# Differential scores with grouped 64-row products, and projections whose arithmetic leaves GpSimd

## Chip, cores and metric

One core of a Trainium2 chip runs the whole kernel. The metric is device microseconds from launch to end. The time before is 1314.98 us, the median of three runs (1313.61 to 1316.22); the execution that was profiled took 1315.7 us.

## The reference, cut to what matters

One layer of a transformer block on 1024 tokens of 1024 columns, in float32. The part around the change:

```python
h = rms_norm(x, norm_mix)
q_lat, kv_lat, k_rope_in, dq, dk, dv, g_mla, g_diff = split(h @ w_in)
# latent attention (8 heads): q and k get a norm with a gain, 32 of 96 columns are rotated
q = rms_norm(rms_norm(q_lat) @ w_uq, q_gain);  k = rms_norm(concat(k_nope, k_rope), k_gain)
# differential attention (4 heads, 2 halves of 64 columns): 16 of 64 columns are rotated
q = rms_norm(dq.reshape(4, 2, 64), q_gain);  k = rms_norm(dk.reshape(4, 2, 64), k_gain)
p1 = softmax(q1 @ k1.T * scale);  p2 = softmax(q2 @ k2.T * scale)   # chunk-causal, blocks of 128 queries
o = rms_norm((p1 - lam * p2) @ v, subln)
# then gates, up-projections, w_out, a router and 32 experts (top 2 in one group)
```

## The kernel before, in words

Every product of two float32 matrices is made of rounded parts (`split`, line 81): ScalarE copies the operand to the rounded type (`hi`), another engine takes the remainder (`lo`), and three products (`mm3`, line 85) are summed in PSUM: hi x hi, hi x lo, lo x hi. A *remainder* below is the TENSOR_TENSOR of line 83. `split` does it on VectorE unless it is given GpSimd; `load_split` (line 148) gives GpSimd all weight pieces but the first, and lines 419 and 422 give it those of `w_uq` and `w_ukv`.

The kernel runs in stages. **Projections** (0 to 285 us): the transposed input is loaded in two halves of tokens (`load_hT`), the norm of each token comes from squares of x (`norm_x`, line 170), and the eight token tiles of the differential queries are made first, into eight PSUM banks (`first`): tiles 0 and 1 share one tile of the pool psA, 2 and 3 the other; tile 4 is in bank "g". `diff_proj` (line 268) empties a bank: a square on ScalarE, a sum over each of 16 half-heads and an inverse root by a Newton step on VectorE, then scaling and rotation. For queries (c = 0) it reads the bank with the product of both gains (`gdqk`, line 285) and with rotary tables (`rope`, line 241, lines 246 to 250), and the norm is applied at the end by GpSimd (line 288). For keys (c = 1) VectorE applies the norm while it reads the bank (lines 293 and 294). Then a loop over tiles (line 426) makes the latents (`lat_proj`, in bank "g" from tile 1 on), the values (`dv_proj`), the latent queries and keys (`prep`, where GpSimd applies the queries' norm in line 401) and their transposes (`turn`, line 255, through PSUM and one ScalarE copy to DRAM). A second loop (line 446) does the differential keys.

**Latent attention** (299 to 487 us) and **differential attention** (487 to 687 us) follow. For each head and block i of 128 queries `diff_scores` (line 637) makes two score matrices of (i + 1) x 128 keys, one for each half f. The halves lie in partitions 0 to 63 and 64 to 127. The first product of a half has 128 rows (hi and lo of the query stacked against hi of the key, line 655), the second one 64 rows (hi of the query against lo of the key, line 656), and up to 512 columns each: one column piece for i below 4, two from there on. For i below 4 both halves lie in one psA tile, from i = 4 on each takes a psA tile of its own; the pool has two. VectorE masks a corner and takes the row maximum (lines 657 and 511), ScalarE the exponential (line 514). Scores are made two blocks ahead of their use; products of the gates (`gates`, lines 86 to 88 with `pG`) are dealt out as filler by `filler`.

What stands in an engine's queue, and in which order, is settled when the kernel is built: a scheduler takes the program's order as priority and a model of times, so that a later instruction whose operands and buffers are free in its model passes an earlier one whose buffer is not.

After 687 us come the output projection, the router and the experts, which the change does not touch.

Of the kernel before, what the change touches and what calls it, by code (L numbers as in the profile page):

```python
# [10 lines left out]
F32 = mybir.dt.float32  # L11
# [4 lines left out]
AF = mybir.ActivationFunctionType  # L16
ALU = mybir.AluOpType
# [7 lines left out]
P = 128  # L25
KD = 8
MH, MN, MR, MV, MQK = 8, 64, 32, 64, 96
# [4 lines left out]
LAMBDA_INIT = 0.8 - 0.6  # L32
NEG = -1e30
N_RAW = 5
SPV = (0,)
XB = 4
XTB = 4
NGB = 4
# [10 lines left out]
def kernel(ctx: ExitStack, tc: tile.TileContext, a, out):  # L49
    nc = tc.nc  # L50
# [97 lines left out]
    def load_split(src, n):  # L148
        i = next(raws)
        raw = er(i)[:, :n]  # L150
        nc.sync.dma_start(raw, src)
        hi = pw.tile([P, 1024], F32R, name="whi", bufs=6)
        lo = pw.tile([P, 1024], F32R, name="wlo", bufs=6)
        split(hi[:, :n], lo[:, :n], raw, None if i in SPV else nc.gpsimd)
        return hi, lo

    gT = p1.tile([P, KD], F32, name="gT")
# [37 lines left out]
    for k2 in range(4):  # L195
        w_dq.append(w_piece(a["w_dqkv"][0], 512, k2))
        for k in (2 * k2, 2 * k2 + 1):
            load_hT(k, 0)
            for t in range(4):
                proj(first[t], t, w_dq, 512, k, k + 1)  # L200
    for k in range(KD):
        load_hT(k, 1)
    norm_x(0, 4)
    norm_x(4, NT)
    first += [bank(x) for x in ("g", "o", "", "")]
    for k in range(KD):
# [34 lines left out]
    def rope(dst, src, tab, t, nh, h, r0):  # L241

        tmp = p1.tile([P, 2, 256], F32, name="rtmp", bufs=2)
        m = [tmp[:, i, :nh * 2 * h].rearrange("p (n h) -> p n h", h=2 * h) for i in range(2)]
        for m_, x in zip(m, tab):
            nc.vector.tensor_tensor(m_, src[:, :, r0:r0 + 2 * h], x[:, t:t + 1, :].to_broadcast([P, nh, 2 * h]),  # L246
                                    op=ALU.mult)
        mc, ms = m
        nc.vector.tensor_tensor(dst[:, :, r0:r0 + h], mc[:, :, :h], ms[:, :, h:], op=ALU.subtract)
        nc.vector.tensor_tensor(dst[:, :, r0 + h:r0 + 2 * h], mc[:, :, h:], ms[:, :, :h], op=ALU.add)  # L250

    def work(name, shape, dt=F32, bufs=2):
        return p1.tile(shape, dt, name=name, bufs=bufs)

    def turn(pool, srcs, dsts, w):

        pt = bank2()
        n = [x.shape[-1] // w for x in srcs]
        for j, (x, b) in enumerate((x, b) for x, n_ in zip(srcs, n) for b in range(n_)):
            nc.tensor.transpose(pt[:w, j * P:(j + 1) * P], x[:, b * w:(b + 1) * w], ident)  # L260
        o = pool.tile([P, KD, P], F32, name="to", bufs=2)
        nc.scalar.activation(o[:w], pt[:w, :].rearrange("p (h n) -> p h n", n=P), AF.Copy)
        h = 0
        for (d_, t_), n_ in zip(dsts, n):
            nc.sync.dma_start(d_[:, :, t_ * P:(t_ + 1) * P], o[:w, h:h + n_, :])
            h += n_

    def diff_proj(c, t, w, ps=None):
        if ps is None:
            ps = bank(("g", "")[t % 2])  # L270
            proj(ps, t, w, 512)
        r_ = rx[:, t:t + 1]
        o = work("v", [P, 512]) if c else px.tile([P, 512], F32, name="v0", bufs=4)
        sq = work("sq", [P, 512], bufs=1)
        nc.scalar.activation(sq, ps, AF.Square, scale=r_)
        ss = work("ss8", [P, 8])
        nc.vector.tensor_reduce(ss, sq.rearrange("p (h d) -> p h d", d=DHD), axis=AX, op=ALU.add)
        r8 = work("r8", [P, 8])
        rstd_newton(p1, r8, ss, DHD)
        src = ps.rearrange("p (h d) -> p h d", d=DHD)  # L280
        ov = o.rearrange("p (h d) -> p h d", d=DHD)
        if c == 0:
            rs = work("rs8", [P, 8])
            nc.vector.tensor_scalar(rs, r8, r_, DHD ** -0.5, op0=ALU.mult, op1=ALU.mult)
            nc.vector.tensor_tensor(ov[:, :, DR:], src[:, :, DR:],
                                    gdqk[:, None, DR:].to_broadcast([P, 8, DHD - DR]), op=ALU.mult)
            rope(ov, src, tdq, t, 8, 8, 0)
            nc.gpsimd.tensor_tensor(ov, ov, rs[:, :, None].to_broadcast([P, 8, DHD]), op=ALU.mult)
            nc.sync.dma_start(dqr_d[t * P:(t + 1) * P, :], o)
        else:  # L290
            nc.vector.tensor_scalar(r8, r8, r_, None, op0=ALU.mult)
            kn = work("kn", [P, 8, DR])
            nc.vector.tensor_tensor(kn, src[:, :, :DR], r8[:, :, None].to_broadcast([P, 8, DR]), op=ALU.mult)
            nc.vector.tensor_tensor(ov[:, :, DR:], src[:, :, DR:],
                                    r8[:, :, None].to_broadcast([P, 8, DHD - DR]), op=ALU.mult)
            rope(ov, kn, tdk, t, 8, 8, 0)
        return o

    gdqk = p1.tile([P, DHD], F32, name="gdqk")
    nc.vector.tensor_tensor(gdqk, gdq, gdk, op=ALU.mult)  # L300
    tdq = tables("tdq", gdq, cd, sd, 0, 8)
    tdk = tables("tdk", gdk, cd, sd, 0, 8)
    for t in range(NT):
        diff_proj(0, t, w_dq, first[t])
    es_x.close()

    gqk = p1.tile([P, MN], F32, name="gqk")
    nc.vector.tensor_tensor(gqk, gq[:, :MN], gk[:, :MN], op=ALU.mult)
    tq = tables("tq", gq, cm, sm, MN, 16)
    tk = tables("tk", gk, cm, sm, MN, 16)  # L310

# [55 lines left out]
    def prep(t):  # L367
# [25 lines left out]
        rstd_newton(p1, r16, ss, MQK)  # L393
        nc.vector.tensor_scalar(r16[:, :8], r16[:, :8], MQK ** -0.5, None, op0=ALU.mult)
        q = pp.tile([P, MH, MQK], F32, name="q", bufs=1)
        for h0, h1, o in ((0, 5, 0), (5, 8, 512)):
            src = pq[:, o:o + (h1 - h0) * MQK].rearrange("p (h d) -> p h d", d=MQK)
            nc.vector.tensor_tensor(q[:, h0:h1, :MN], src[:, :, :MN],
                                    gqk[:, None, :].to_broadcast([P, h1 - h0, MN]), op=ALU.mult)
            rope(q[:, h0:h1, :], src, tq, t, h1 - h0, 16, MN)  # L400
        nc.gpsimd.tensor_tensor(q, q, r16[:, :8, None].to_broadcast([P, MH, MQK]), op=ALU.mult)
        kk = pp.tile([P, MH, MQK], F32, name="k", bufs=1)
        rk = r16[:, 8:16, None]
        nc.vector.tensor_tensor(kk[:, :, :MN], pk.rearrange("p (h d) -> p h d", d=MN),
                                rk.to_broadcast([P, MH, MN]), op=ALU.mult)
        nc.vector.scalar_tensor_tensor(kk[:, :, MN:], kr.to_broadcast([P, MH, MR]), rx[:, t:t + 1],
                                       rk.to_broadcast([P, MH, MR]), op0=ALU.mult, op1=ALU.mult)
        QK[t] = ((q, q_d), (kk, k_d))

    QK = {}  # L410

    def prep_t(t):
        for x, d_ in QK.pop(t):
            turn(pp, [x.rearrange("p h d -> p (h d)")], [(d_, t)], MQK)

    for k in range(2):
        raw = er(next(raws))[:, :768]
        nc.sync.dma_start(raw, a["w_uq"][:, k, :])
        split(uqh[:, k, :], uql[:, k, :], raw, nc.gpsimd)
    raw = er(next(raws))  # L420
    nc.sync.dma_start(raw, a["w_ukv"])
    split(ukh, ukl, raw, nc.gpsimd)
    w_dv = dv_pieces(0)
    early = [bank2()]
    early = [x[:, o:o + 512] for o in (0, 512) for x in early]
# [20 lines left out]
    for t in range(NT):  # L446
        dk = diff_proj(1, t, w_dk)
        dv_proj(1, t, w_dv, bank("o"))
        if t:
            turn(pt_, [fetch("dqr", dqr_d, t - 1, 2), dk_], [(dq_d, t - 1), (dk_d, t - 1)], P)  # L450
        dk_ = dk
    turn(pt_, [fetch("dqr", dqr_d, t, 2), dk_], [(dq_d, t), (dk_d, t)], P)
    es_1.close()
    es_w.close()

# [181 lines left out]
    def diff_scores(m):  # L637

        h, i = divmod(m, NT)
        qs, ks, kl, _ = HD["d", h]  # L640
        n = (i + 1) * P
        ps = bank2()
        if i < 4:
            ps, cuts = [ps[:, :512], ps[:, 512:]], [slice(0, n)]
        else:
            (p0, cuts), (p1, _) = score_banks(ps, i), score_banks(bank2(), i)
            ps = [p0, p1]
        r_ = pa.tile([P, 2], F32, name="rd", bufs=4)
        s_ = pa.tile([P, 2], F32, name="sd", bufs=4)
        p = []  # L650
        for f in range(2):
            c = slice(f * 64, f * 64 + 64)
            q = qs[f][:, i * P:(i + 1) * P]
            for k in cuts:
                nc.tensor.matmul(ps[f][:, k], q, ks[f][:, k], start=True, stop=False)
                nc.tensor.matmul(ps[f][:, k], q[c], kl[c, k], start=False, stop=True)
            nc.vector.memset(ps[f][0:64, n - 64:n], NEG)
            p.append(softmax_exp(pa, ps[f], n, f"d{f}", s_[:, f:f + 1])[0])
        nc.vector.reciprocal(r_, s_)
        p_1, r_1 = p[0], r_[:, 0:1]  # L660
# [587 lines left out]
```

## Time and profile before

| | |
|---|---|
| median of three runs | 1314.98 us |
| the profiled execution | 1315.7 us |
| its span, first to last instruction | 1313.6 us |
| TensorE busy | 1193.0 us (91%) |
| VectorE busy | 943.8 us (72%) |
| ScalarE busy | 735.1 us (56%) |
| GpSimd busy | 233.0 us (18%) |

In the profile's rows PE is TensorE, PEld its weight loads, DVE VectorE, ACT ScalarE, POOL GpSimd. L83 is line 83 of the kernel. A row of a line names what it writes and reads. Matmul ends are modelled and overlap with the next one, so the distance between starts says what a product costs. [...]

### The profile page before, as it was taken

The numbers are of one execution on the slowest core, as the hardware profiler recorded it, in microseconds if no ns is written. First come the engines' busy times: TensorE is split into PE (matmuls) and PEld (weight loads), VectorE is DVE, ScalarE is ACT, GpSimd is POOL, SyncE is SP. The second block draws the span as 40 slices with busy tenths as digits, with TensorE's granted clock in tenths as the row PEclk, the third lists the DMA queues.
The fourth block names the chain that finished last, engine by engine and source line by source line (L and its number), as shares of the span: only waits on it lengthen the run. The fifth ranks groups of instructions, "written<-read, shape, count | busy, mean of one in ns | idle before, by whom it ended". The sixth has DMA issues, their size and how long they took to land. (4 is left out here: it accounts for less than half of the span.)

```text
span 1313.6 us, 18269 instructions
## 1 busy us (share of the span) xinstructions
PE 1193.0 (91%) x6105; PEld 954.1 (73%) x6105; DVE 943.8 (72%) x2071; ACT 735.1 (56%) x1368; POOL 233.0 (18%) x175
## 2 busy tenths in 40 slices
PE   7769969999999999999999899999599989899994
PEld 6668858877888886666778678888477756666773
DVE  5487685447888887877675678445679878878992
ACT  5444443246676675766565444211478767677882
POOL 2341050010000001101010000000154434342111
PEclk9889979999999999999999999999689989999997
DMA  8843346475233323313114443754569999999993
GB/s 263 200 155 116 105 124 173 122 154 121 78 92 94 88 81 113 102 60 96 65 33 137 152 144 113 267 181 169 199 194 342 309 311 303 327 317 343 341 319 56
DMA packets 107423, 228.61 MB, mean 174 GB/s; under 512 B 13793, under 2 KB 47201, under 8 KB 107329
## 3 DMA queue, kind: packets, MB, share of 16 engines
q1 hardware_dynamic: 86272, 201.98, 46.1%
q0 software_dynamic: 21056, 25.46, 9.6%
q8 instruction: 49, 0.80, 0.3%
q14 instruction: 46, 0.37, 0.1%
HBM read 187.53 MB, written 52.43 MB: 183 GB/s over the span
## 5 line engine op out<-in xcount | busy, mean ns | idle before, releaser
L83 DVE TENSOR_TENSOR elo<-ring,ehi 128x1024 fp32r<-128x1024 f32 x120 | 141.8, 1220 | 16.2 <-ACT ehi L82 15.9
L82 ACT ACTIVATE ehi<-ring 128x1024 fp32r<-128x1024 f32 x120 | 124.8, 1058 | 33.9 <-DMA ring<-in_w_exp 16.6
L514 ACT ACTIVATE pd<-pA,nbd 128x512 f32<-128x512 f32 (+7 forms) x128 | 94.7, 740 | 33.9 <-DVE nbd L511 33.0
L86 PE MATMUL pG<-ring,whi 128*128 128x512 f32 x240 | 101.2, 422 | 4.0 <-ACT sg L488 3.8
L511 DVE TENSOR_REDUCE nbd<-pA 128x1 f32<-128x128 f32 (+7 forms) x128 | 95.7, 748 | 4.1 <-PE pA L562 3.5
L87 PE MATMUL pG<-ring,whi 128*128 128x512 f32 x240 | 97.3, 406 | 0.0
L88 PE MATMUL pG<-ring,wlo 128*128 128x512 f32 x240 | 97.0, 404 | 0.0
L83 DVE TENSOR_TENSOR elo<-er,ehi 128x1024 fp32r<-128x1024 f32 x72 | 85.5, 1220 | 9.7 <-ACT ehi L82 9.5
L82 ACT ACTIVATE ehi<-er 128x1024 fp32r<-128x1024 f32 x72 | 75.0, 1058 | 21.4 <-DMA er<-in_w_exp 8.0
L1083 POOL DMA_INDIRECT out<-y,ids x22 | 54.1, 2457 | 143.3 <-DVE elo L83 30.6
L86 PE MATMUL pG<-ehi,xh 128*112 128x512 f32 x128 | 53.0, 414 | 20.5 <-ACT xh L82 20.5
L523 PE MATMUL pB<-ident,pd 128*128 128x128 f32 x432 | 66.5, 278 | 1.3 <-DVE pt L83 0.2
L86 PEld LDWEIGHTS pG<-ring,whi 128*128 128x128 f32 x240 | 46.2, 193 | 16.5 <-ACT sg L488 7.0
L523 PEld LDWEIGHTS pB<-ident,pd 128*128 128x128 f32 x432 | 48.9, 141 | 12.3 <-issue 2.6
L86 PE MATMUL pG<-whi,ring 128*128 128x416 f32 (+1 forms) x96 | 37.5, 391 | 21.5 <-DVE rtmp L246 20.8
L88 PE MATMUL pB<-ehi,ehl 128*112 128x512 f32 x128 | 54.7, 427 | 1.8 <-DVE ehl L83 1.8
L86 PE MATMUL pB<-ehi,ehh 128*112 128x512 f32 x128 | 54.8, 428 | 0.9 <-DVE y L1082 0.7
L82 ACT ACTIVATE whi<-er 128x512 fp32r<-128x512 f32 (+2 forms) x48 | 36.0, 758 | 31.0 <-PE pG L87 11.6
L88 PEld LDWEIGHTS pG<-ring,wlo 128*128 128x128 f32 x240 | 46.0, 192 | 10.0 <-issue 0.4
L87 PE MATMUL pB<-elo,ehh 128*112 128x512 f32 x128 | 53.0, 414 | 0.0
L88 PE MATMUL pG<-ehi,xl 128*112 128x512 f32 x128 | 52.0, 406 | 0.0
L87 PEld LDWEIGHTS pG<-ring,whi 128*128 128x128 f32 x240 | 46.2, 192 | 7.6 <-issue 1.0
(391 smaller groups left out, 3569.0 us busy)
## 6 DMA issues: line engine op xcount, KB each, us to landing
ring<-in_w_exp SPq DMA_DIRECT2D x120, 512.0 KB
er<-in_w_exp SPq DMA_DIRECT2D x72, 512.0 KB
er<-in_w_gate SPq DMA_DIRECT2D x16, 512.0 KB
g_d<-sg SPq DMA_DIRECT2D x32, 256.0 KB
sgl<-g_d SPq DMA_DIRECT2D x32, 256.0 KB
er<-in_w_dqkv SPq DMA_DIRECT2D x8, 512.0 KB
xT<-in_xT SPq DMA_DIRECT2D x16, 256.0 KB
xt<-in_x SPq DMA_DIRECT2D x8, 512.0 KB
```

Of the source, the lines that this page charges most:

```text
L82: nc.scalar.activation(hi, src, AF.Copy)
L83: (eng or nc.vector).tensor_tensor(lo, src, hi, op=ALU.subtract)
L86: nc.tensor.matmul(ps, ah, bh, start=start, stop=False)
L87: nc.tensor.matmul(ps, ah, bl, start=False, stop=False)
L88: nc.tensor.matmul(ps, al, bh, start=False, stop=stop)
L511: nc.vector.tensor_reduce(nb, ps[:, :n], axis=AX, op=ALU.max, negate=True)
L514: nc.scalar.activation(p[:, :n], ps[:, :n], AF.Exp, bias=nb, accum_out=s)
L523: nc.tensor.transpose(pt[:, (b - b0) * P:(b - b0 + 1) * P], p[:, b * P:(b + 1) * P], ident)
L1083: nc.gpsimd.indirect_dma_start(out=out[:, :], out_offset=bass.IndirectOffsetOnAxis(ap=idx[:BT, :], axis=0), in_=y[:BT, :], in_offset=None, ...
```

## The change

Two changes are put together.

In `diff_scores` the 128-row products of both halves come first, then the 64-row products, in turn for half 0 and half 1 of each column piece; mask and softmax of both halves follow all products.

In the projections no arithmetic is given to GpSimd any more. All weight remainders go to VectorE. `diff_proj` reads queries the way it reads keys: the norm is applied while the bank is read, with a copy `kn` (now one buffer) of the 16 columns to be rotated. `prep` does the same with `qn`, and rotates eight heads at once. The product of both gains for the columns that are not rotated becomes a column (`gain_column`, small loads on GpSimd's DMA queue) and is the scale of the ScalarE copy in `turn`; for the differential part that copy becomes two, one for queries and one for keys. `norm_x(0, 4)` comes ahead of the second half of `load_hT`.

```diff
-SPV = (0,)
...
-        split(hi[:, :n], lo[:, :n], raw, None if i in SPV else nc.gpsimd)
+        split(hi[:, :n], lo[:, :n], raw)
...
+    norm_x(0, 4)
     for k in range(KD):
         load_hT(k, 1)
-    norm_x(0, 4)
     norm_x(4, NT)
...
-            nc.vector.tensor_tensor(m_, src[:, :, r0:r0 + 2 * h], x[:, t:t + 1, :].to_broadcast([P, nh, 2 * h]),
-                                    op=ALU.mult)
+            nc.vector.tensor_tensor(m_, src, x[:, t:t + 1, :].to_broadcast([P, nh, 2 * h]), op=ALU.mult)
...
+    def gain_column(nm, gains, cuts, n):
+
+        col_ = p1.tile([P, 2], F32, name=f"{nm}2")
+        nc.vector.memset(col_, 1.0)
+        for i, g_ in enumerate(gains):
+            for p0, d0, d1 in cuts:
+                nc.gpsimd.dma_start(col_[p0:p0 + d1 - d0, i:i + 1], a[g_][d0:d1].rearrange("(p o) -> p o", o=1))
+        r = p1.tile([P, 1], F32, name=nm)
+        nc.vector.tensor_tensor(r[:n], col_[:n, 0:1], col_[:n, 1:2], op=ALU.mult)
+        return r
+
-    def turn(pool, srcs, dsts, w):
+    def turn(pool, srcs, dsts, w, gains):
...
-        nc.scalar.activation(o[:w], pt[:w, :].rearrange("p (h n) -> p h n", n=P), AF.Copy)
         h = 0
-        for (d_, t_), n_ in zip(dsts, n):
+        for (d_, t_), n_, g_ in zip(dsts, n, gains):
+            src = pt[:w, h * P:(h + n_) * P].rearrange("p (h n) -> p h n", n=P)
+            if g_ is None:
+                nc.scalar.activation(o[:w, h:h + n_, :], src, AF.Copy)
+            else:
+                nc.scalar.activation(o[:w, h:h + n_, :], src, AF.Copy, scale=g_[:w])
             nc.sync.dma_start(d_[:, :, t_ * P:(t_ + 1) * P], o[:w, h:h + n_, :])
...
+        nc.vector.tensor_scalar(r8, r8, r_, DHD ** -0.5 if c == 0 else 1.0, op0=ALU.mult, op1=ALU.mult)
+        kn = work("kn", [P, 8, DR], bufs=1)
+        nc.vector.tensor_tensor(kn, src[:, :, :DR], r8[:, :, None].to_broadcast([P, 8, DR]), op=ALU.mult)
+        nc.vector.tensor_tensor(ov[:, :, DR:], src[:, :, DR:],
+                                r8[:, :, None].to_broadcast([P, 8, DHD - DR]), op=ALU.mult)
+        rope(ov, kn, (tdk if c else tdq), t, 8, 8, 0)
         if c == 0:
-            rs = work("rs8", [P, 8])
-            nc.vector.tensor_scalar(rs, r8, r_, DHD ** -0.5, op0=ALU.mult, op1=ALU.mult)
-            nc.vector.tensor_tensor(ov[:, :, DR:], src[:, :, DR:],
-                                    gdqk[:, None, DR:].to_broadcast([P, 8, DHD - DR]), op=ALU.mult)
-            rope(ov, src, tdq, t, 8, 8, 0)
-            nc.gpsimd.tensor_tensor(ov, ov, rs[:, :, None].to_broadcast([P, 8, DHD]), op=ALU.mult)
             nc.sync.dma_start(dqr_d[t * P:(t + 1) * P, :], o)
...
-    gdqk = p1.tile([P, DHD], F32, name="gdqk")
-    nc.vector.tensor_tensor(gdqk, gdq, gdk, op=ALU.mult)
+    gdqk = gain_column("gdqk", ("dq_gain", "dk_gain"), ((DR, DR, DHD), (DHD + DR, DR, DHD)), P)
...
-    gqk = p1.tile([P, MN], F32, name="gqk")
-    nc.vector.tensor_tensor(gqk, gq[:, :MN], gk[:, :MN], op=ALU.mult)
+    gqk = gain_column("gqk", ("mq_gain", "mk_gain"), ((0, 0, MN),), MQK)
...
+        qn = work("qn", [P, MH, MR], bufs=1)
         for h0, h1, o in ((0, 5, 0), (5, 8, 512)):
             src = pq[:, o:o + (h1 - h0) * MQK].rearrange("p (h d) -> p h d", d=MQK)
-            nc.vector.tensor_tensor(q[:, h0:h1, :MN], src[:, :, :MN],
-                                    gqk[:, None, :].to_broadcast([P, h1 - h0, MN]), op=ALU.mult)
-            rope(q[:, h0:h1, :], src, tq, t, h1 - h0, 16, MN)
-        nc.gpsimd.tensor_tensor(q, q, r16[:, :8, None].to_broadcast([P, MH, MQK]), op=ALU.mult)
+            rq = r16[:, h0:h1, None]
+            nc.vector.tensor_tensor(q[:, h0:h1, :MN], src[:, :, :MN], rq.to_broadcast([P, h1 - h0, MN]), op=ALU.mult)
+            nc.vector.tensor_tensor(qn[:, h0:h1, :], src[:, :, MN:], rq.to_broadcast([P, h1 - h0, MR]), op=ALU.mult)
+        rope(q, qn, tq, t, MH, 16, MN)
...
-        split(uqh[:, k, :], uql[:, k, :], raw, nc.gpsimd)
+        split(uqh[:, k, :], uql[:, k, :], raw)
...
-    split(ukh, ukl, raw, nc.gpsimd)
+    split(ukh, ukl, raw)
...
+        qs = [x[:, i * P:(i + 1) * P] for x in qs]
         for f in range(2):
-            c = slice(f * 64, f * 64 + 64)
-            q = qs[f][:, i * P:(i + 1) * P]
             for k in cuts:
-                nc.tensor.matmul(ps[f][:, k], q, ks[f][:, k], start=True, stop=False)
-                nc.tensor.matmul(ps[f][:, k], q[c], kl[c, k], start=False, stop=True)
+                nc.tensor.matmul(ps[f][:, k], qs[f], ks[f][:, k], start=True, stop=False)
+
+        for k in cuts:
+            for f in range(2):
+                c = slice(f * 64, f * 64 + 64)
+                nc.tensor.matmul(ps[f][:, k], qs[f][c], kl[c, k], start=False, stop=True)
+        for f in range(2):
             nc.vector.memset(ps[f][0:64, n - 64:n], NEG)
             p.append(softmax_exp(pa, ps[f], n, f"d{f}", s_[:, f:f + 1])[0])
```

## Rows read from the trace of the kernel before

**Rows 1.** The page's first part: busy time of each engine, share of the span, instructions.

```profile
PE 1193.0 (91%) x6105; PEld 954.1 (73%) x6105; DVE 943.8 (72%) x2071; ACT 735.1 (56%) x1368; POOL 233.0 (18%) x175
```

**Rows 2.** Busy time by stretch: stretch, length, PE, PEld, DVE, ACT, POOL, PEclk, DMA share, GB/s.

```profile
8.00:54.15 46.15, 46.15 (x192) 37.54 (x191) 22.68 (x37) 27.02 (x42) 17.30 (x9) 1.00 0.87 238
54.15:61.09 6.94, 0.00 (x2) 0.03 (x1) 4.24 (x20) 1.56 (x3) 1.26 (x2) 0.78 0.67 179
67.54:73.71 6.17, 0.00 (x1) 0.04 (x1) 6.17 (x13) 2.19 (x4) 4.93 (x3) 0.83 0.40 131
73.71:83.51 9.80, 9.80 (x48) 9.35 (x48) 9.69 (x46) 4.80 (x19) 4.10 (x5) 0.76 0.45 162
174.34:187.07 12.73, 0.00 (x2) 0.03 (x1) 12.34 (x17) 3.87 (x6) 11.58 (x6) 0.62 0.14 46
187.07:192.00 4.93, 4.93 (x16) 4.17 (x17) 1.01 (x4) 0.00 (x0) 0.30 (x1) 0.59 0.59 160
```

**Rows 3.** Waits of TensorE, 0 to 300 us: total us, times, longest.

```profile
PE pG L86 <- DVE rtmp L246: 20.8, 5, 12.7
```

**Rows 4.** VectorE in order of time: start, duration, instruction, what ended idle time.

```profile
10.28 2.36 DVE L167 SCALAR_TENSOR_TENSOR ring<-xT,gT,ring 128x512 fp32r<-128x512 f32 x1 [1.07 <-ACT ring L166]
...
173.16 0.16 DVE L123 SCALAR_TENSOR_TENSOR rsn<-rsn 128x16 f32<-128x16 f32 x1
...
183.60 2.27 DVE L349 TENSOR_SCALAR rl<-rl,rx 128x2 f32<-128x2 f32 x1
```

**Rows 5.** GpSimd in order of time, 168 to 187 us.

```profile
176.60 9.25 POOL L83 TENSOR_TENSOR wlo<-er,whi 128x1024 fp32r<-128x1024 f32 x4
```

**Rows 6.** Busy time of the differential scores' stage, summed over its eight parts.

```profile
sum 192.50, PE 188.49 PEld 133.06 DVE 145.43 ACT 121.92 POOL 21.67; mean PE 23.56 PEld 16.63 DVE 18.18 ACT 15.24 POOL 2.71
```

**Rows 7.** TensorE's products in order of time, head 0, i = 5.

```profile
518.14 0.45 PE L655 MATMUL pA<-x,x 128*128 128x512 f32 x1
518.51 0.49 PE L656 MATMUL pA<-x,x 64*128 64x512 f32 x1
518.94 0.38 PE L655 MATMUL pA<-x,x 128*128 128x256 f32 x1
519.25 0.38 PE L656 MATMUL pA<-x,x 64*128 64x256 f32 x1
519.56 0.50 PE L87 MATMUL pG<-ring,whi 128*128 128x512 f32 x1
...
520.37 0.39 PE L87 MATMUL pG<-ring,whi 128*128 128x512 f32 x1
520.60 0.28 PE L709 MATMUL pO<-er,at 128*128 128x256 f32 x1
520.72 0.40 PE L88 MATMUL pG<-ring,wlo 128*128 128x512 f32 x1
...
521.18 0.39 PE L655 MATMUL pA<-x,x 128*128 128x512 f32 x1
```

**Rows 8.** Groups by line, 0 to 300 us: count, busy us, mean ns, idle before.

```profile
L83 POOL TENSOR_TENSOR wlo<-er,whi 128x1024 fp32r<-128x1024 f32 x11 | 26.4, 2417 | 22.3 <-ACT whi L82 22.3
...
L83 DVE TENSOR_TENSOR wlo<-er,whi 128x1024 fp32r<-128x1024 f32 x1 | 1.2, 1225 | 5.7 <-ACT whi L82 5.7
...
L293 DVE TENSOR_TENSOR kn<-pB,r 128x128 f32<-128x128 f32 x4 | 1.2, 292 | 0.1
```

**Rows 9.** VectorE in order of time: the first rotary table and its last use, tile 0.

```profile
57.03 0.29 DVE L235 TENSOR_TENSOR tdqc<-cd,gdq 128x128 f32<-128x128 f32 x1 [2.70 <-DMA cd<-in_cos_d]
...
58.05 0.28 DVE L246 TENSOR_TENSOR rtmp<-pA,tdqs 128x128 f32<-128x128 f32 x1
```

**Rows 10.** ScalarE in order of time: pieces 8 and 9 of 16 of the input.

```profile
18.31 1.34 ACT L166 ACTIVATE ring<-xT,gT 128x512 fp32r<-128x512 f32 x2 [1.52 <-DMA xT<-in_xT]
```

**Rows 11.** Groups by line, whole span: the exponentials of both attentions.

```profile
L514 ACT ACTIVATE pd<-pA,nbd 128x512 f32<-128x512 f32 (+7 forms) x128 | 94.7, 740 | 33.9 <-DVE nbd L511 33.0
...
L514 ACT ACTIVATION_READ_ACCUMULATOR pd<-pA,nbd 128x1 f32 x128 | 25.4, 198 | 0.0
```

More of the change, by code (lines that the diff above doesn't have):

```diff
@@ L281, in diff_proj @@
         ov = o.rearrange("p (h d) -> p h d", d=DHD)
-        if c == 0:
-            rs = work("rs8", [P, 8])
-            nc.vector.tensor_scalar(rs, r8, r_, DHD ** -0.5, op0=ALU.mult, op1=ALU.mult)
-            nc.vector.tensor_tensor(ov[:, :, DR:], src[:, :, DR:],
-                                    gdqk[:, None, DR:].to_broadcast([P, 8, DHD - DR]), op=ALU.mult)
-            rope(ov, src, tdq, t, 8, 8, 0)
-            nc.gpsimd.tensor_tensor(ov, ov, rs[:, :, None].to_broadcast([P, 8, DHD]), op=ALU.mult)
-            nc.sync.dma_start(dqr_d[t * P:(t + 1) * P, :], o)
[L290 to L296, printed above, removed]
-        return o
-    gdqk = p1.tile([P, DHD], F32, name="gdqk")
-    nc.vector.tensor_tensor(gdqk, gdq, gdk, op=ALU.mult)
+        nc.vector.tensor_scalar(r8, r8, r_, DHD ** -0.5 if c == 0 else 1.0, op0=ALU.mult, op1=ALU.mult)
[4 more added lines that the diff above has]
+        rope(ov, kn, (tdk if c else tdq), t, 8, 8, 0)
+        if c == 0:
+            nc.sync.dma_start(dqr_d[t * P:(t + 1) * P, :], o)
+        return o
+    gdqk = gain_column("gdqk", ("dq_gain", "dk_gain"), ((DR, DR, DHD), (DHD + DR, DR, DHD)), P)
     tdq = tables("tdq", gdq, cd, sd, 0, 8)
@@ L407, in prep @@
                                        rk.to_broadcast([P, MH, MR]), op0=ALU.mult, op1=ALU.mult)
-        QK[t] = ((q, q_d), (kk, k_d))
+        QK[t] = ((q, q_d, gqk), (kk, k_d, None))
     QK = {}
     def prep_t(t):
-        for x, d_ in QK.pop(t):
-            turn(pp, [x.rearrange("p h d -> p (h d)")], [(d_, t)], MQK)
+        for x, d_, g_ in QK.pop(t):
+            turn(pp, [x.rearrange("p h d -> p (h d)")], [(d_, t)], MQK, [g_])
     for k in range(2):
@@ L449 @@
         if t:
-            turn(pt_, [fetch("dqr", dqr_d, t - 1, 2), dk_], [(dq_d, t - 1), (dk_d, t - 1)], P)
+            turn(pt_, [fetch("dqr", dqr_d, t - 1, 2), dk_], [(dq_d, t - 1), (dk_d, t - 1)], P, [gdqk, None])
         dk_ = dk
-    turn(pt_, [fetch("dqr", dqr_d, t, 2), dk_], [(dq_d, t), (dk_d, t)], P)
+    turn(pt_, [fetch("dqr", dqr_d, t, 2), dk_], [(dq_d, t), (dk_d, t)], P, [gdqk, None])
     es_1.close()
```

## The prediction

> **What bounds the kernel now.** I read the page first: TensorE has work for 91% of the span [rows 1], so a change counts where TensorE has none, or where its products take longer than their columns. Next came the table of busy time by stretch for the projections (0 to 285 us). It shows three holes of TensorE: 6.94 us from 54.15, 6.17 us from 67.54 and 12.73 us from 174.34, and behind each a stretch at a lower granted clock: 0.76 from 73.71 to 83.51, 0.59 from 187.07 to 192 [rows 2]. The list of waits names who ends them: most of it is L246 of VectorE (the last read of a PSUM bank that the next product needs), 20.8 us in 5 waits [rows 3]. Then the same stretch in order of time, for VectorE and GpSimd side by side. From 168 to 186 VectorE looks busy, but seven of its small instructions take 2 us more than their like: L349 on 2 columns needs 2.27 us and ends at 185.87 with the fourth of GpSimd's remainders, where L123 on 16 columns has 0.16 us while GpSimd is idle [rows 4, 5]. From 10.28 to 183.60 I count 23 VectorE instructions stretched that way, 33 us in all, each beside a TENSOR_TENSOR of GpSimd. GpSimd's arithmetic thus stops VectorE, and VectorE stops TensorE.
>
> In the differential attention (487.5 to 680 us) it is the other way round: TensorE is busy 188.5 of 192.5 us, VectorE 145.4 [rows 6]. There I read the products in order of time. A 128-row product of 512 columns is followed by the next 0.23 us later, one of 256 columns 0.12 us later. Around a 64-row product that isn't so: 128x512 to 64x512 takes 0.37 us, on to the next 128 rows 0.43, then 0.31 and 0.31 for 256 columns [rows 7]. Four products that stream in 0.70 us take 1.42, so each trip to 64 rows and back costs (1.42 - 0.70)/2 = 0.36 us. There are 96 such trips (4 heads x 2 halves x 12 pieces): 35 us.
>
> **The change part by part. Grouped products.** With i below 4 both halves share one PSUM tile, so the four products follow each other: 1 trip in place of 2. With i of 4 and more, each half has a PSUM tile of its own, and the pool has two. The second half's tile comes free only after the exponential of the block before. The rows show what TensorE does then: the second half starts at 521.18, 1.6 us after the first half made way at 519.56, and gate products fill the time [rows 7]. I expect the same: the first half's 64-row products are ready, the second half's 128-row ones are not, so they go first and the halves stay apart. That is 2 trips in place of 4 (each half's two 64-row products now stand together). Trips saved: 16 x 1 + 16 x 2 = 48, at 0.36 us 17.3 us. The bounds: if the halves also stay together from i = 4 on, 64 trips or 23 us, and with products of both halves running at once another half of 36,864 columns at 0.23 us per 512, 8.3 us, so 31 us. If a change between the two halves' rows costs a trip too, nothing is gained below i = 4 and 11.5 us remain. The nearest rows (products 128 rows after 128 rows) speak for no cost between them, and no row shows two at once. TensorE is 98% busy there, VectorE has 47 us free [rows 6]; I let a tenth be lost to waits: **16 us**.
>
> 128-row products of one kind follow each other at 0.23 us for 512 columns, with a weight load for each [rows 7]. [...]
>
> **Arithmetic from GpSimd to VectorE.** GpSimd loses 18 weight remainders (12 of 1024 columns at 2.4 us, 6 narrower), 8 of L288 and 8 of L401. VectorE gets the remainders: at 1.22 us for 1024 columns at most 18 x 1.22 = 22 us, and 8 copies `kn` for the queries, 0.29 us each, 2.3 us [rows 8]. In `prep` the scaled rotary part is two reads more, but `rope` then runs once for 8 heads in place of twice: no change within 0.1 us. So VectorE gets at most 24 us of work and loses 33 us of standstill. The gains in the ScalarE copy of `turn` ride on an existing instruction; 8 copies become two of half size, under TensorE's work after 210 us. The gain columns are 6 small DMAs on GpSimd's queue, needed 40 us later; with that cover gone they would delay one turn by some us, once.
>
> *At 54 us.* The bank is let go after the rotary tables: their cosine lands at 57.03 [rows 9], which the change does not move. With `kn` and the rest read as soon as the norm is known, block 0 leaves its bank early; block 1's `kn` waits for the one `kn` buffer, which block 0's two table products free at 58.33 [rows 9]; 0.3 us later TensorE can start, at 58.7 in place of 61.09: 2.4 us. *At 67 us.* From block 0's last table product (58.05) to the end of the hole (73.71) four blocks take 15.6 us, of which 5.2 are standstill: 2.6 each. In the change they need 0.3 more for `kn`, but the norms of blocks 1 and 2 (some 1.5 us each) no longer stand behind the tables: 58.3 + 4 x 2.9 - 3 = 67, with a remainder of w_dv between them perhaps 68 in place of 73.71. Since the hole begins 2.4 us earlier too, that is 6 us up to here and a hole of 3. Of the clock stretch behind (9.80 us at 0.76, 2.4 us lost) I count 1. VectorE then is the one in line up to 86 us, with 3 remainders of w_uq and w_ukv, so nothing more. *At 174 us.* The standstills go (13.5 us), six remainders come (7.3 us), in the gaps of a chain (square, norm, scaling) which had 3.5 us in the earlier rounds. I take a hole of 3 us in place of 12.73, and the 2 us that the clock of 0.59 takes from the 4.93 us behind. Sum 6 + 1 + 9.7 + 2 = 18.7, taken as **18 us**. Bounds: all holes of rows 2 with their clocks gone, 26 + 4 = 30 us; remainders all in line with TensorE, 33 - 24 = 9 less the new waits, say 5 us.
>
> *The norm moved ahead.* Its 4 loads of 512 KB, 4 squares on ScalarE and the small write now pass 8 loads of xT on SP's queue. At 238 GB/s [rows 2] 2 MB are 8.8 us. The second half of xT is first needed when 96 products are through, 8 + 96 x 0.23 = 30 us; its first piece is in its high part by 19.65 now [rows 10]: covered, 10 us against 8.8. Without that cover it would cost what lies over. The norm comes earlier, but the tables bind: 0.
>
> The sum is against the profiled execution: 1315.7 us (span 1313.6, 2.1 us around it), 0.7 above the median of the three runs. 1315.7 - 16 - 18 = 1281.7; less 0.7, **1281 us**. Everything behind 680 us (out, router, experts) moves earlier as a whole, DMAs too, since its loads start from TensorE's progress.
>
> **Rivals.** *Both halves at once (0.20).* The scheduler keeps the halves together also above i = 4 and the array runs them side by side: 31 us less a tenth, 28, and the 18 of the projections: 1269 us. For it: different rows, different PSUM banks. Against: the gap at 519.56. [...]
>
> *VectorE takes the holes over (0.19).* The remainders land in its queue ahead of the norm chain, the holes stay half open: 6 us in the projections, 14 in the scores: 1295 us. For it: VectorE was in line at every hole. Against: it loses more standstill than it gains work.
>
> *Slower: products and exponentials stand in line with VectorE (0.06).* If the order puts all products of a block ahead of both reductions and the next block behind both exponentials, VectorE stands for the products (1.4 us) and one exponential (0.74 + 0.20 us [rows 11]) in each block: 145.4 + 32 x 2.35 = 220.6 us for this stage, 28 more than 192.5. Less 18 that is 1325 us. It decides from a standstill of VectorE of (47.1 + 18)/32 = 2.03 us a block; now it is 1.47. Against: gate products and two blocks ahead keep the order loose.
>
> *The products don't come together (0.02).* Order unchanged, and VectorE only swaps waits: 1314 us.
>
> **How the numbers follow.** The forecast has 0.53, its own range 1272 to 1290. From 1265 (both halves at once) to 1299 (holes taken over) 8 in 10 are held. Differences under 0.2% (2.6 us) can't be told from none. Faster 0.92 (forecast and the first two rivals), within 0.2% 0.02 (the last), slower 0.06.
>
> **What would show it.** In the profile after: no GpSimd TENSOR_TENSOR before 285 us, no VectorE instruction of 16 columns over 0.5 us, the hole at 174 under 4 us, the one at 67 under 4. In the scores, below i = 4 two 64-row products in a row; from i = 4 on, two of one half, and 48 trips in all; the stage of 192.5 us at about 176. Wrong would be: a stage over 185 us, or holes of TensorE before 285 us of over 20 us in sum.

## The result and the profile after

The changed kernel takes 1281.72 us (median of four runs, 1276.85 to 1282.23) beside 1314.42 us for the kernel before in the same comparison: a ratio of 0.9741, 95% interval 0.9715 to 0.9767, or 33 us. The prediction was 1281. A second comparison, made later beside other experiments, gave 1284.12 against 1317.62: 0.9757 (0.9727 to 0.9788). The profiled execution took 1276.85 us (span 1275.1) and so lies 5 us under its median; what two traces of this kernel differ by, and where, is shown further down.

The first part of the page answers to [rows 1]: TensorE is busy 26 us less, VectorE 6, GpSimd 64.5.

```profile
PE 1166.7 (92%) x6105; PEld 941.1 (74%) x6105; DVE 937.7 (74%) x2083; ACT 735.6 (58%) x1376; POOL 168.5 (13%) x147
```

The table by stretch answers to [rows 2] and [rows 6]; the columns are the same (stretch, length, busy time of PE, PEld, DVE, ACT and POOL with counts, the clock granted to TensorE as a share of the full one, DMA share, GB/s). The traces of the kernel before and of the changed one record two levels of it, 1.00 and 0.50; a row has the mean over its stretch.

```profile
53.67:60.97 7.30, 0.00 (x0) 0.03 (x1) 2.81 (x13) 0.00 (x0) 0.00 (x0) 0.71 0.60 121
68.45:73.21 4.76, 0.00 (x2) 0.03 (x1) 4.55 (x14) 2.84 (x6) 0.00 (x0) 1.00 0.54 171
73.21:82.42 9.21, 9.21 (x48) 8.80 (x48) 7.96 (x48) 3.80 (x17) 0.00 (x0) 0.81 0.39 144
168.49:169.45 0.96, 0.00 (x0) 0.00 (x1) 0.96 (x2) 0.96 (x4) 0.00 (x0) 1.00 0.08 30
169.45:176.00 6.55, 6.55 (x40) 5.66 (x41) 5.85 (x17) 3.90 (x7) 0.76 (x1) 1.00 0.45 123
464.10:640.20 176.10, 170.55 (x910) 126.58 (x909) 146.63 (x388) 121.48 (x329) 21.72 (x35) 0.99 0.30 86
```

The hole of 12.73 us is down to 0.96 us, and the clock behind it is full (1.00; 0.59 before). The holes at 54 and 68 us, however, are still there (7.30 and 4.76 us; 6.94 and 6.17 before). The stage of the differential scores has gone from 192.5 to 176.1 us. TensorE's three longest waits for VectorE up to 285 us answer to [rows 3] (total us, times, longest): L245 is the old L246 and keeps 1.5 of its 20.8 us, while L298 (the scaled read of a bank) is new.

```profile
PE pA L85 <- DVE v L298: 7.3, 1, 7.3
PE pG L85 <- DVE v L298: 4.8, 1, 4.8
PE pG L85 <- DVE rtmp L245: 1.5, 3, 0.5
```

Half of the hole at 68 us is remainders. VectorE has two of them, of w_dv, in its queue ahead of the read that ends the hole (start, duration):

```profile
68.63 1.23 DVE L82 TENSOR_TENSOR wlo<-er,whi 128x1024 fp32r<-128x1024 f32 x1 [0.95 <-ACT whi L81]
...
70.91 1.22 DVE L82 TENSOR_TENSOR wlo<-er,whi 128x1024 fp32r<-128x1024 f32 x1
...
72.51 0.55 DVE L298 TENSOR_TENSOR v<-pG,r 128x384 f32<-128x384 f32 x1
```

VectorE around the old hole, in order of time, answers to [rows 4, 5]. L353 on 2 columns is the old L349: 0.22 us in place of 2.27. The remainders (L82) now stand in this queue at 1.2 us each (three in these rows), and TensorE is at work again from 169.45.

```profile
168.44 1.20 DVE L82 TENSOR_TENSOR wlo<-er,whi 128x1024 fp32r<-128x1024 f32 x1
...
170.63 1.21 DVE L82 TENSOR_TENSOR wlo<-er,whi 128x1024 fp32r<-128x1024 f32 x1
171.76 0.22 DVE L353 TENSOR_SCALAR rl<-rl,rx 128x2 f32<-128x2 f32 x1
171.89 1.21 DVE L82 TENSOR_TENSOR wlo<-er,whi 128x1024 fp32r<-128x1024 f32 x1
```

TensorE's products of a block i = 5 answer to [rows 7] (L659 is the 128-row product, L664 the 64-row one, x2 two in a row). Each half has its own group: 128, 128, 64, 64 rows, then other work, then the second half.

```profile
492.77 0.61 PE L659 MATMUL pA<-x,x 128*128 128x512 f32 x2
493.31 0.62 PE L664 MATMUL pA<-x,x 64*128 64x512 f32 x2
493.86 0.50 PE L85 MATMUL pG<-ring,whi 128*128 128x512 f32 x1
494.20 0.22 PE L720 MATMUL pO<-er,at 128*128 128x128 f32 x1
494.26 0.56 PE L659 MATMUL pA<-x,x 128*128 128x512 f32 x2
494.75 0.62 PE L664 MATMUL pA<-x,x 64*128 64x512 f32 x2
495.29 0.39 PE L718 MATMUL pO<-er,at 128*128 128x256 f32 x1
```

To see where the time went, I compare the start of TensorE's n-th product in the traces. The table says by how many us it comes earlier than in the kernel before, at six points of that kernel's time and at the end of the span.

| trace | 82 us | 161 us | 192 us | 276 us | 484 us | 692 us | span |
|---|---|---|---|---|---|---|---|
| changed | 1.1 | 5.8 | 19.8 | 20.7 | 23.4 | 38.9 | 38.5 |
| changed, second time | -1.1 | 3.9 | 17.9 | 18.1 | 18.8 | 36.8 | 34.9 |
| scores alone | 1.8 | 0.5 | 0.9 | 1.1 | 1.6 | 19.0 | 17.6 |
| projections alone | 0.4 | 5.5 | 19.5 | 17.7 | 17.4 | 14.3 | 13.9 |
| remainders alone | 2.0 | 5.6 | 18.6 | 18.4 | 19.9 | 19.3 | 17.8 |

Two stretches carry the gain: 161 to 192 us (13 to 14 us, in every trace with the remainders moved) and 484 to 692 us (15 to 18 us in the three traces here with grouped products, 13 to 18 in all eleven). Two traces of the same changed kernel differ by 4.6 us at 484 us: 1.9 us are there by 161 us, and most of the rest comes between 264 and 300 us, where the second waits longer for the first exponential of the latent attention (3.0 us, 1.4 in the first) and then has a granted clock of 0.88 from 280 to 300 us (1.00 in the first).

### The profile page after: what moved, and what is told of

Same layout as the page of the kernel before. It is cut to its first block, busy times and chain, and to the rows that moved or that the text cites. A ratio compares the mean times of both kernels' runs of the same rounds, so it can differ in the third digit from the quotient of the medians.

```text
span 1275.1 us, 18222 instructions
## 1 busy us (share of the span) xinstructions
PE 1166.7 (92%) x6105; PEld 941.1 (74%) x6105; DVE 937.7 (74%) x2083; ACT 735.6 (58%) x1376; POOL 168.5 (13%) x147
## 4 chain that ended last, share of the span: by engine, by line
PE 49%; DMA 29%; DVE 12%; ACT 5%; issue 3%; SPq 1%; POOL 0%; POOLq 0%; ACTq 0%; DVEq 0%
DMA ring<-in_w_exp 12%; DMA er<-in_w_exp 7%; PE pG L85 6%; PE pG L86 5%; PE pG L87 5%; PE pA L85 3%; PE pB L528 3%; PE pA L86 3%; PE pA L87 3%; DMA sgl<-g_d 2%; PE pO L87 2%; PE pO L85 2%; PE pO L86 2%; DVE nbd L516 2%; PE pA L664 1%
## 5 line engine op out<-in xcount | busy, mean ns | idle before, releaser
L82 DVE TENSOR_TENSOR elo<-ring,ehi 128x1024 fp32r<-128x1024 f32 x120 | 142.4, 1220 | 16.2 <-ACT ehi L81 15.3
L516 DVE TENSOR_REDUCE nbd<-pA 128x1 f32<-128x512 f32 (+7 forms) x128 | 95.4, 748 | 3.3 <-PE pA L567 2.6
L82 DVE TENSOR_TENSOR elo<-er,ehi 128x1024 fp32r<-128x1024 f32 x72 | 85.7, 1219 | 13.5 <-ACT ehi L81 13.3
L85 PE MATMUL pG<-ehi,xh 128*112 128x512 f32 x128 | 52.5, 410 | 18.6 <-ACT xh L81 18.6
L85 PEld LDWEIGHTS pG<-ring,whi 128*128 128x128 f32 x240 | 45.4, 189 | 17.5 <-ACT sg L493 6.7
L86 PE MATMUL pO<-elo,xh 128*112 128x512 f32 x128 | 50.6, 395 | 2.5 <-DVE elo L82 2.5
L85 PE MATMUL pO<-ehi,xh 128*112 128x512 f32 x128 | 51.7, 404 | 0.7 <-ACT ehi L81 0.7
## 6 DMA issues: line engine op xcount, KB each, us to landing
ring<-in_w_exp SPq DMA_DIRECT2D x120, 512.0 KB, 13.7
```

The lines of the kernel that those rows point to most:

```text
L85: nc.tensor.matmul(ps, ah, bh, start=start, stop=False)
L86: nc.tensor.matmul(ps, ah, bl, start=False, stop=False)
L516: nc.vector.tensor_reduce(nb, ps[:, :n], axis=AX, op=ALU.max, negate=True)
```

## The experiments

Each was timed in five rounds beside the kernel before; ratios are to it. Differences under some 0.3% aren't told apart by these times, so most readings rest on the traces.

### Each part alone

The grouped products put into the kernel before (`diff_scores` of the change, nothing else):

> The kernel before with the grouped 64-row products alone. If the two parts add up, as the prediction took it: nothing moves ahead of 485 us, the stage of the differential scores goes from 192.5 to about 176 us, and the time is 1314.4 - 16 = 1298 us. Rival, the gain of the scores depends on the projections (or the other way round): the stage stays over 182 us and the time over 1304 us.

Measured: 1298.66 us, 0.9864 (0.9833 to 0.9896). The stage is 172.9 us from its first score product to its last, in place of 191.3, and nothing moves ahead of it (1.6 us at 484 us).

The projections alone (the change with the old order of the products):

> The changed kernel with the old order of the products in the differential scores. By the traces (TensorE's work at 484 us is 23.4 us earlier in the changed kernel) 1314.4 - 23 = 1291 us; by the 18 us of the prediction 1296 us. The hole at 54 us stays at 7 us, the one at 68 us at 4 to 5, none at 174 us over 1 us. If the parts don't add up: over 1300 us.

Measured: 1295.39 us, 0.9836 (0.9805 to 0.9868). The kernel before took 1317.83 us in this comparison, so the part gives 21.6 us, uncertain by 4, which can't tell the 18 us of the prediction from the 23 of one trace. The score stage is 194.4 us long here, 3.1 more than before. The lower granted clock accounts for that:

```profile
490.00:500.00 10.00, 9.46 (x22) 5.88 (x22) 4.99 (x14) 5.02 (x13) 0.55 (x1) 0.53 0.17 46
```

That is 4.7 us lost, where the kernel before has 0.93 from 500 to 510 us and 0.90 from 510 to 520, 1.7 us. The product of the two ratios is 0.970, uncertain by 0.004; the whole gave 0.974 and 0.976, each uncertain by 0.003. By the traces 17.4 us at 484 us in this kernel and 17.4 from 484 to 692 us in the other make 34.8, where the whole has 36.8 and 38.9 at 692 us (the 3 us that this kernel loses behind 484 us are the clock's and left out): the parts add up within what can be told.

### Which of GpSimd's products counted

The kernel before, with all weight remainders on VectorE and GpSimd's other sixteen products (L288, L401) left where they were:

```diff
-        split(hi[:, :n], lo[:, :n], raw, None if i in SPV else nc.gpsimd)
+        split(hi[:, :n], lo[:, :n], raw)
...
-        split(uqh[:, k, :], uql[:, k, :], raw, nc.gpsimd)
+        split(uqh[:, k, :], uql[:, k, :], raw)
```

> The kernel before with all weight remainders on VectorE; GpSimd keeps its other products (L288, L401), the scores stay as before. If the standstill beside remainders made the hole at 174 us: it falls from 12.7 to under 2 us, with 2 to 3 us of the waits near 91 to 106 us, and nothing at 54 and 68: 14 to 17 us faster than before, 0.987 to 0.989 of it. Rival, VectorE takes the holes over with the six remainders in front of its norm chain: hole at 174 over 5 us, under 8 us faster, over 0.993.

Measured: 1298.72 us, 0.9867 (0.9838 to 0.9896), 17.5 us. By the table it is 18.4 us ahead at 276 us, as much as all of the projections' edits (17.7 to 20.7). Its four longest waits of TensorE for VectorE up to 264 us (L246 and L83 are lines of the kernel before):

```profile
PE pO L87 <- DVE wlo L83: 5.2, 1, 5.2
PE pA L86 <- DVE rsn L123: 5.0, 1, 5.0
PE pG L86 <- DVE r L124: 2.5, 1, 2.5
PE pG L86 <- DVE rtmp L246: 1.5, 3, 0.5
```

The hole at 174 us is gone (0.95 us from 168.77). One new wait, 5.2 us at 72 us, is for a remainder that now waits its turn on VectorE: at 80 us this kernel is 8.6 us ahead, at 82 us only 2.0. The rival that VectorE takes the holes over is true at that place, and in the changed kernel for half of the hole at 68 us. Sixteen products stay on GpSimd and still stretch eleven VectorE instructions by 7.3 us in all, but only two of these, 0.95 us, lie in a hole of TensorE. So the remainders are the edit that counts; the sixteen products, norm, gains and `kn` together bring nothing that these times can tell.

### What holds TensorE at 54 us

The edit: gains and rotary tables are loaded ahead of the second four loads of x and the latent weights.

```diff
+    gdq = vec("gdq", "dq_gain", DHD)
...
+    for t_, n_ in ((cd, "cos_d"), (sd, "sin_d"), (cm, "cos_m"), (sm, "sin_m")):
+        nc.sync.dma_start(t_, a[n_])
     norm_x(4, NT)
...
     w_lat = w_pieces(a["w_lat"], WL)
-    gdq = vec("gdq", "dq_gain", DHD)
```

> The changed kernel with the loads of gains and rotary tables ahead of the second four loads of x and of the latent weights in SP's queue (they were behind them). If the tables' landing at 58 us sets the holes at 54 and 68 us: block 0 is rotated by 40 us, block 1 leaves its bank at about 52, the hole at 54 goes (7.3 us), that at 68 shrinks to 2 or less, some 1.5 us of the low clock behind them with it: 9 to 12 us faster, 1270 to 1273 us. Rival, VectorE's chain for the blocks sets them: the hole moves to 60 to 68 us and the gain is under 3 us, over 1279 us.

Measured: 1279.11 us, 0.9710 (0.9680 to 0.9741). The first table product starts at 41.07 us in place of 58.10 and TensorE runs on to 57.85: the tables did set the hole at 54. The 9 to 12 us that were expected don't come, since what comes next is the rival's chain. Four of the waits up to 280 us:

```profile
PE pG L85 <- DVE v L298: 4.6, 1, 4.6
PE pA L565 <- ACT pd L519: 3.6, 1, 3.6
PE pB L365 <- DVE lat L355: 3.0, 1, 3.0
PE pO L85 <- ACT sq L347: 2.2, 1, 2.2
```

By 161 us this kernel is 10.0 us ahead of the kernel before, 4.2 more than the changed one; by 484 us it is 22.6 ahead, between the two traces of the changed kernel. At 271 us TensorE waits 3.6 us for the first exponential of the latent attention (1.4 and 3.0 us in the two traces of the changed kernel), and that for q and k: their load was issued at 264.33 in place of 268.10, but landed at 273.37 in place of 274.58.

Four buffers of `kn` in place of one, the tables where the change has them:

> The changed kernel with four buffers of kn for the differential queries in place of one. If the one buffer holds the bank of block 1 (its copy waits for block 0's products with the rotary tables, which land at 58 us), the bank comes free at about 52 us and the hole from 53.67 goes; but the loads of w_dv stand in SP's queue behind the write of block 0's rotated rows at 60.19, so TensorE stands again some 7 us later: 2 to 5 us faster, 1277 to 1280 us. Rival, the hole is set by VectorE's amount of work: hole and time stay, 1282 us.

Measured: 1279.89 us, 0.9715 (0.9688 to 0.9743). The hole at 54 goes here too, and one of 12.55 us comes at 57.22, for the bank of block 4, with VectorE busy 10.12 us of it:

```profile
57.22:69.77 12.55, 0.01 (x1) 0.04 (x1) 10.12 (x46) 3.29 (x7) 0.00 (x0) 0.69 0.79 245
```

Both together:

> Both edits, tables ahead and four kn buffers. If the tables alone bind, nothing is added to the edit of the tables: within 1 us of it. If kn still binds between blocks 1 to 4, 2 to 4 us faster than it.

Measured: 1281.20 us, 0.9723 (0.9697 to 0.9750): nothing is added to the tables alone. With the tables there in time, one `kn` is enough.

The first four loads of x and their norm put back behind the second half of the transposed input:

> The changed kernel with the first four loads of x and their norm back behind the second half of the transposed input, where they were before. If the prediction was right that the tables bind, not the norm: the hole at 54 us stays at 7 us, the time within 2.6 us of the changed kernel. Rival, the earlier norm carries part of the gain: block 0 and 1 leave their banks later, the hole at 54 grows by 2 us or more, over 1285 us.

Measured: 1280.33 us, 0.9730 (0.9701 to 0.9759), not told apart from the change. The rival falls, and the trace says more: the tables come earlier without the move. VectorE's first table product and the read that lets block 1's bank go, in the second trace of the changed kernel and then with the norm put back (start, duration):

```profile
61.03 0.29 DVE L234 TENSOR_TENSOR tdqc<-cd,gdq 128x128 f32<-128x128 f32 x1 [7.54 <-DMA cm<-in_cos_m]
63.05 0.55 DVE L298 TENSOR_TENSOR v<-pA,r 128x384 f32<-128x384 f32 x1
```

```profile
55.30 0.29 DVE L234 TENSOR_TENSOR tdqc<-cd,gdq 128x128 f32<-128x128 f32 x1 [3.91 <-DMA cm<-in_cos_m]
57.34 0.55 DVE L298 TENSOR_TENSOR v<-pA,r 128x384 f32<-128x384 f32 x1
```

In four traces with the norm behind (three of them of kernels with the projections' order of before) the first table product starts at 53.3 to 57.0 us; in seven with it ahead and the tables behind, at 56.6 to 61.0. In six of these seven the hole at 54 ends 2.7 to 4.6 us after that product (in the seventh, the four buffers, it isn't there). It was 10.57 us long in the second trace of the changed kernel and 4.30 with the norm put back. At 161 us the kernel with the norm put back is 9.4 us ahead of the kernel before, 3 to 5 us more than the six traces with the projections of the change as they are (3.9 to 6.2). Later waits take most of that back (21.0 us at 484 us): with the norm put back, the read of `dqr` at 197.60 holds TensorE for 2.56 us, and the clock behind it is 0.83.

```profile
197.60:200.16 2.56, 0.00 (x1) 0.04 (x1) 0.03 (x1) 0.00 (x0) 0.00 (x0) 1.00 1.07 245
200.16:210.00 9.84, 9.84 (x56) 8.96 (x57) 2.31 (x9) 2.64 (x5) 0.00 (x0) 0.83 0.39 112
```

### Trips, or products at once

Below i = 4 the changed kernel's two 64-row products, one of each half, start 3 to 4 ns apart. To take that away and keep the trips:

```diff
-                c = slice(f * 64, f * 64 + 64)
+                c = slice(f * 64, f * 64 + 64) if i >= 4 else slice(0, 64)
```

> The changed kernel, but for blocks below i = 4 the 64-row product of the second half takes its rows from partitions 0 to 63, as that of the first half does (the scores of the second half are then other numbers). Trips, lengths and order stay. If products on different rows run at once (the two start 3 ns apart in the changed kernel), this takes it away: 5,120 columns at 0.23 us per 512 are 2.3 us, and with 0.1 us for each of 16 weight loads 3.9: 1284 to 1286 us, the two starts 0.34 us apart for 512 columns. Rival, the start times are an artefact and only trips count: no change, 1282 us, the stage still 176 us.

Measured: 1280.69 us, 0.9732 (0.9697 to 0.9767). One block i = 3 of the changed kernel, and the same one with the same rows:

```profile
475.61 0.62 PE L659 MATMUL pA<-x,x 128*128 128x512 f32 x2
476.17 0.50 PE L664 MATMUL pA<-x,x 64*128 64x512 f32 x2
476.63 0.38 PE L718 MATMUL pO<-er,at 128*128 128x256 f32 x1
```

```profile
476.14 0.62 PE L659 MATMUL pA<-x,x 128*128 128x512 f32 x2
476.69 0.73 PE L664 MATMUL pA<-x,x 64*128 64x512 f32 x2
477.35 0.39 PE L718 MATMUL pO<-er,at 128*128 128x256 f32 x1
```

From the first 64-row product to the next work 0.46 us pass in the one and 0.66 in the other: products on different rows do run at once. TensorE's steps into, within and out of all score products sum to 56.8 us in the one and 58.7 in the other, and the two kernels differ in 16 such pairs only. The stage, from first to last score product, is 173.6 us with the same rows, 174.8 in the first trace of the changed kernel and 172.3 in the second. The first of these lost 1.7 us to the lower clock, the other two had all of it; the rows are those of the changed kernel's first and second trace:

```profile
476.00:490.00 14.00, 11.80 (x49) 8.20 (x48) 10.82 (x31) 8.28 (x22) 1.87 (x3) 0.88 0.62 169
```

```profile
476.00:490.00 14.00, 13.29 (x71) 9.69 (x70) 11.57 (x35) 9.54 (x27) 2.07 (x3) 1.00 0.60 163
```

Five traces of these scores at full clock have 172.3 to 174.1 us, so whether the 1.9 us come out at the stage's end can't be told. They are some 12% of the stage's gain of 16.4 us; the rest goes with the trips.

The halves forced together from i = 4 on as well, by an order given to the scheduler (the first 64-row product behind the last 128-row one):

```diff
+                if last is not None:
+                    tc.add_manual_dep(mm.ins, last.ins.name, mybir.DependencyInfo(
+                        mybir.DependencyClass.NoSync, mybir.DependencyReason.DATA), reason="pair")
+                    last = None
```

> The changed kernel with the first 64-row product of a block put behind the last 128-row one of both halves, so that the halves stand together from i = 4 on too. If trips and products at once set the time: 16 trips fewer at 0.36 us are 5.8 us, 13,312 columns at once 6.0 us, together 11.8 us, some of it lost to waits: 1270 to 1275 us, 34 runs of 64-row products. Rival, the second half's PSUM tile comes free too late: TensorE stands (idle 5.6 us in this stage now, over 15 then), the stage is over 180 us and the time over 1286 us.

Measured: 1280.54 us, 0.9725 (0.9695 to 0.9755), with four 64-row products in a row. The stage from first to last score product, in the changed kernel 174.8 us with TensorE busy for 169.3, and the longest wait in it:

```profile
466.80:641.90 175.10, 160.83 (x907) 120.76 (x905) 147.04 (x383) 119.39 (x327) 30.56 (x35) 0.99 0.30 86
```

```profile
PE pB L740 <- DVE dof L734: 9.2, 17, 2.3
```

TensorE's steps around the score products fall by 7.5 us, its idle time rises by 8.7. The saving is real and turns into waits, most of them for VectorE's `dof`. Both expectations had one half of that right. GpSimd has a part in it: its busy time in the stage rises from 21.5 to 30.6 us with the same 35 instructions. The inverse root that `dof` needs (L108, one column, 0.55 us in the median of the changed kernel) takes 1.06 to 1.92 us in twelve blocks, each time beside VectorE's L676. One of them (start, duration):

```profile
507.57 1.15 DVE L676 SCALAR_TENSOR_TENSOR pd<-pd,lr,pd 128x896 f32<-128x896 f32 x1
507.79 1.34 POOL L108 TENSOR_TENSOR drs<-dss,neghalf 128x1 f32<-128x1 f32 x1 [5.74 <-DVE dss L107]
509.17 0.35 DVE L734 TENSOR_SCALAR dof<-dof,drs,rd 128x128 f32<-128x128 f32 x1 [0.45 <-POOL drs L108]
```

VectorE itself stands 10.5 us in front of `dof` (22 times) until that root is there. What the root on VectorE would give wasn't tried.

The turning of a block's output (L740, L736 in the changed kernel) put one block later, so that it doesn't wait:

```diff
-LAGO = 1
+LAGO = 2
```

> Forced pairs, and the turning of a block's output (L736) put one block later in TensorE's queue (LAGO 2 in place of 1). With forced pairs TensorE's steps around the score products fell by 7.5 us, but its idle time rose from 5.6 to 14.3 us, 9.2 of it in front of L740 by VectorE's dof. If only the place of that transpose in the queue binds: idle falls to 6 us and the stage from 175 to about 167 us, 1273 to 1276 us. Rival, VectorE itself is the bound of the stage: the wait appears in front of the next block's products or values, stage over 172 us, time over 1278 us.

Measured: 1284.14 us, 0.9739 (0.9713 to 0.9765). The wait for `dof` is gone, and the idle time isn't (14.8 us):

```profile
469.30:643.60 174.30, 159.53 (x906) 118.94 (x904) 147.01 (x383) 118.24 (x326) 28.41 (x35) 1.00 0.30 87
```

```profile
PE pA L659 <- ACT pd L519: 5.6, 9, 1.3
PE pB L528 <- DVE pd L676: 2.1, 3, 1.3
PE pO L722 <- ACT at L81: 1.2, 1, 1.2
```

Now the next block's products wait for the exponential that frees their PSUM tile, as the rival had it. With pairs forced, waits for the engines behind TensorE take back what it saves; whether more PSUM would give the 8 us back wasn't tried.

> The same with the gains and rotary tables loaded ahead too: the 4 us that the tables gave by 250 us were lost again up to 282 us, where the first q and k of the latent attention land. If that repeats: within 2 us of the run without it. If the 4 us stay: 4 us faster.

Measured: 1279.89 us, 0.9713 (0.9687 to 0.9739): the tables' gain of 4 us up to 161 us is lost again up to 484 us (21.1 us ahead there). None of these versions can be told from the changed kernel by its time.

The changed kernel beside the last three:

> The changed kernel once more, beside the next three: 0.974 of the kernel before, 1281 to 1283 us, as the first runs of it; a run on another chip may put all times up or down by 0.3%.

Measured: 1284.12 us, 0.9757, as told above; the profiled execution has the holes at 54 and 71 us with 10.57 and 4.20 us, and none over 1 us at 174. Its score stage is 172.3 us from first to last score product.

## Why the prediction was right, and where its steps were not

**Grouped products: 16 us forecast, 16.4 measured** (stage 192.5 to 176.1; 18 in the trace with them alone). The step holds as it stood. Below i = 4 all four products come together, from i = 4 on each half by itself, and 96 trips became 50 where 48 were forecast (two groups are split by another product). From first to last score product 191.3 us became 174.8; by 46 trips that is 0.36 us each, the price read from [rows 7]. That it fits so closely is in part luck: TensorE's steps around score products fell by more, from 79.5 to 56.8 us, and the rest of the stage took 6 us back. The running of two halves at once, which the prediction counted in a rival only, is there below i = 4 (3 to 4 ns between the two starts) and is worth 1.9 us of TensorE's steps, too little to be told at the stage's end. What makes a trip cost 0.36 us, no run shows. Between two 64-row products of one half the prediction counted no cost, and there is one: in the trace of the changed kernel the second starts 0.33 to 0.34 us after the first at 512 columns (23 pairs), where most gate products of 128 rows have 0.23. Score products of 128 rows lie between (0.23 to 0.34, 26 pairs). Where the 0.1 us come from, no run tells.

**Projections: 18 us forecast, 18 to 21 in the traces at 276 us, 21.6 ± 4 in the time of that part alone.** The sum is right and its terms are not; that they make up for each other is luck.
- *At 174 us*, 11.7 us with the clock: 14.0 measured (5.8 to 19.8 us ahead). The remainders fit into the gaps of the chain, and the hole of 3 us that was left for them is 0.96.
- *At 54 us*, 2.4 us: 0.1, and 2.7 us lost in the second trace. The step failed where it took the tables' landing as fixed at 57.03: with the norm moved ahead they came some 3 us later (four traces beside seven; 1.1 us in the first trace), and four table products and two parts of `rope` went ahead of block 1's read. "The norm moved ahead: 0" was wrong by as much at this place, and right in the time, since later waits took it back.
- *At 67 us*, 6 us in all: 0.5. The hole ends at 73.21 where 68 was forecast. 1.2 us come from the step before (block 0's last table product ends at 59.55, not at 58.33). From there 13.7 us pass, not 9.7: two remainders of w_dv stand ahead of the read where one was counted (1.2 us), and VectorE stands 0.95 us for the operand of the first; the other 2 us aren't taken apart. The clock behind it gave 0.6 where 1 was counted.
- *Behind 84 us*, nothing: 4.5 us from 82 to 111 us. "Nothing more" overlooked that TensorE waited 0.87 and 0.64 us for remainders of w_uq and w_ukv on GpSimd; with the remainders alone some 3 us come there too.

By its own marks, three are met (no GpSimd product before 285 us, no stretched instruction, the hole at 174) and two missed: the hole at 68 is 4.76 us, not under 4, and the holes before 285 us, the start left out, sum to some 23 us where over 20 was to count as wrong.

**The rivals.** Both halves at once: the mechanism works when forced, and its 12 us don't come, since TensorE's steps fall by 7.5 us and its waits for the other engines rise by 8.7. VectorE takes the holes over: for half of the hole at 68 us. The standstill of the slow rival never came; VectorE's idle time in the stage is 29 us, 0.9 a block, under its 2.03. Behind 680 us all moved nearly as a whole, as forecast (38.9 us at 692 and 38.5 at the end in the first trace, 36.8 and 34.9 in the second).

## What to carry to other kernels

Count changes between 128 and 64 rows, not products: a trip from 128 to 64 rows and back cost 0.36 us here, and what putting more products of one kind together saves on TensorE can come back as waits for the engines behind it (7.5 us saved, 8.7 us waited). Before moving arithmetic between engines, find which instructions stand still beside it and which of these the critical engine waits for: 18 remainders mattered, 16 other products on GpSimd could not be told from nothing. Moved arithmetic takes its place in another queue, here 2.4 us of a hole. A wait that ended with a small load (7.30 us at 54 us) went when the load moved up in the queue; the 4.2 us gained by 161 us could no longer be told at 484 us (22.6 us ahead there, beside 23.4 and 18.8 in the two traces of the change). Look at the granted clock before two lengths of a stage are compared: it made 3 us of difference here.

## What the runs showed of the hardware

A VectorE instruction on 2 columns (L349 of the kernel before) took 2.27 us beside a 128x1024 TENSOR_TENSOR of GpSimd, and has 0.22 us without one in the changed kernel (L353). The other way round, a TENSOR_TENSOR of GpSimd on one column took 1.06 to 1.92 us beside VectorE's SCALAR_TENSOR_TENSOR on 640 to 1024 columns (L676, twelve times, with the halves forced together), and has 0.55 us in the median of the changed kernel. Two 64-row products on different halves of the rows start 3 to 4 ns apart; at 512 columns 0.46 us pass from the first of them to the next work, and 0.66 us where both are on the same half. Small table loads behind large ones were ready anywhere from 53 to 61 us in eleven traces; 58.1 and 61.0 in the two of the changed kernel, which differ by 1.9 us at 161 us.
